# Split weights in a ring whose places begin 64 bytes further, modulo 512, from one to the next

## The chip, the cores and the metric

The kernel runs on one core of one Trainium2 chip. The metric is the device time of one execution in microseconds. Three runs of the kernel before took 1205.24, 1208.13 and 1209.83 us (median 1208.13).

## The reference

Two layers over 512 latent tokens of width 1024, with 256 context tokens. Layer 0 mixes tokens by windowed grouped-query attention (16 heads of 64), layer 1 by a short gated convolution. Each layer ends with a ConvFFN of width 2816. Cut to what carries the time:

```python
def short_conv_mixer(a, w_in, conv_w, w_out):
    gate_b, gate_c, u = jnp.split(a @ w_in, 3, axis=-1)
    return (gate_b * dwconv3(gate_c * u, conv_w)) @ w_out

def conv_ffn(a, w_up, conv_w, w_down):
    g, u = jnp.split(dwconv3(a @ w_up, conv_w), 2, axis=-1)
    return (jax.nn.silu(g) * u) @ w_down

# every layer, latent tokens
sh1, sc1, g1, sh2, sc2, g2 = adaln(c, ada_w[i], ada_b[i])
h = h + g1 * mixer(modulate(rms_norm(h, norm_mix[i]), sh1, sc1))
h = h + g2 * conv_ffn(modulate(rms_norm(h, norm_ffn[i]), sh2, sc2), ffn_w_up[i], ffn_conv[i], ffn_w_down[i])
```

All inputs and the output are float32.

## The kernel before

Activations stand transposed, features on the 128 partitions and tokens along the free dimension. Each float32 operand of a large product is split in two parts of type `fp32r`: `hi` is the rounded value, `lo` what is left. A product of one 128x128 block of weights with 512 (or 256) tokens is then three matmuls, `mm3` (L198 to L201): `hi` x `hi`, `hi` x `lo`, `lo` x `hi`. Each of them loads its block of weights anew; the block is 128 columns of 4 bytes, 512 bytes on each partition.

Weights come from HBM in pieces of 128x1024 (4096 bytes on each partition). `wraw` (L173) loads a piece on SP's queue into one of four buffers. `wpiece` (L180) then splits it: ScalarE writes `whi` (L167), VectorE writes `wlo` (L168). These two go to a ring of places. Ring A has four places for `whi` and four for `wlo` in the pool `ring`; from the FFN pool on, ring B adds three of each, and the pieces use the seven in turn. In the start and in attention pieces of `wqkv` are split into ring A, and there they are the streamed operand (L285 to L287) and the activations are the loaded one.

Ahead of these rings stands the pool `const`: `par`, a tile `pad` that nothing reads, `ident`, `ones`, small columns; then `work` with the 4 buffers of `t` and the 18 of `g`; then `ring` with 4 `wraw`, 4 `whi`, 4 `wlo`. Pools of the stages follow: `e`, then `start` and later `attn`, which are closed before the FFN pool opens in their room. The FFN pool holds `h` (8), ring B (3 `whi`, 3 `wlo`), `crow`, `f` (10), `a` (16), `araw` (3), in this order of addresses. Tiles are laid one behind the other, and so the size of `pad` sets where all that follow in `const`, `work` and `ring` begin.

The order of the work is written out in `START` and `ORDER` for the first layer's attention; from the FFN pool on it is the order of the loops in `out_proj`, `ffn` and the short convolution. `proj` (L721) runs the 24 matmuls of one output block of 128 features. During the first layer's FFN GpSimd and ScalarE compute the second layer's modulation columns from `araw` tiles (L696, L708), two tiles for each step of the FFN.

The lines of before that the change touches:

```python
PAD = 176
    cp.tile([P, PAD], F32, name="pad")
        hi = p.tile([P, 1024], F32R, tag="whi" + t, name=nm("whi"), bufs=nb)
        lo = p.tile([P, 1024], F32R, tag="wlo" + t, name=nm("wlo"), bufs=nb)
```

Of the kernel before, what the change touches and what calls it, by code (L numbers as in the profile page):

```python
# [8 lines left out]
F32R = mybir.dt.float32r  # L9
# [5 lines left out]
P = 128  # L15
# [16 lines left out]
WIN0 = (0, 0, 1, 2)  # L32
WINN = (4, 5, 5, 4)
MASK0 = (5, 2, 2, 0)
HOOK_AT = 6
HALF_AT = 2
KEY_BLOCKS = ((0, 2), (0, 3), (0, 4), (0, 4), (1, 4), (2, 4))
# [8 lines left out]
NPC = _n  # L46
NPC0 = PC["gffn"][0]
NPC1 = PC["qn"][0]
PAD = 176

# [44 lines left out]
def kernel(ctx: ExitStack, tc: tile.TileContext, xT, ctxT, par_d, rope_d, mask_d, ident_d,  # L97
# [11 lines left out]
    def nm(s):  # L109
        uid[0] += 1  # L110
        return f"{s}{uid[0]}"
# [30 lines left out]
    par = cp.tile([P, NPC1], F32, name="par")  # L142
    cp.tile([P, PAD], F32, name="pad")
    ident = cp.tile([P, P], F32, name="ident")
# [21 lines left out]
    def split(raw, hi, lo):  # L166
        act.copy(out=hi, in_=raw)  # L167
        vec.tensor_tensor(out=lo, in0=raw, in1=hi.bitcast(F32), op=ALU.subtract)  # L168
# [4 lines left out]
    def wraw(src, n=1024):  # L173
        raw = rg.tile([P, 1024], F32, tag="wraw", name=nm("wraw"), bufs=4)
        sp.dma_start(out=raw[:, :n], in_=src)
        return raw
# [3 lines left out]
    def wpiece(src, n=1024, raw=None):  # L180
        raw = wraw(src, n) if raw is None else raw
        p, t = ring_pools[wcount[0] % len(ring_pools)]
        nb = sum(r[1] == t for r in ring_pools)
        wcount[0] += 1
        hi = p.tile([P, 1024], F32R, tag="whi" + t, name=nm("whi"), bufs=nb)
        lo = p.tile([P, 1024], F32R, tag="wlo" + t, name=nm("wlo"), bufs=nb)
        parts = 1
        if splits[0] > 0:
            splits[0] -= 1
        elif splits[1] > 0:  # L190
            splits[1] -= 1
            parts = 2
        for i in range(0, n, n // parts):
            cl = slice(i, i + n // parts)
            split(raw[:, cl], hi[:, cl], lo[:, cl])
        return hi, lo
# [71 lines left out]
    with ExitStack() as attn:  # L268
# [22 lines left out]
        with tc.tile_pool(name="start", bufs=1, reuse_waits="tile") as st:  # L291
# [36 lines left out]
            def split_w(i):  # L328
                kvw.append(wpiece(None, 1024, kvraw[i]))
# [234 lines left out]
        def M(p, b, t):  # L564
            e, s = es[p, b, t]
            n = WINN[b] * P
            np_, w = (1, 512) if n == 512 else (2, 320)
            mb = mask[:, MASK0[b]:MASK0[b] + WINN[b], :].rearrange("p a b -> p (a b)")
            h = 2 * p + t
# [114 lines left out]
    with tc.tile_pool(name="ffn", bufs=1, reuse_waits="tile") as fp, four_banks() as sp3:  # L684
# [36 lines left out]
        def proj(pieces, ah, al, halves=False, group=None, hook=None):  # L721
# [5 lines left out]
            for hf in (HALVES if halves else (FULL,)):  # L727
                for m0 in range(0, n, group):
                    for kt in range(nk):
                        if hook is not None and kt == HOOK_AT and hf.start == 0:  # L730
                            hook()
# [12 lines left out]
        for m in range(KT):  # L744
            t = fp.tile([P, 512], F32, tag="h", name=nm("h"), bufs=8)
# [14 lines left out]
        def out_proj(src, n, ah, al, gate, nxt=None, last=False, lead=(), tail_w=None, after=None, cols=None):  # L760
# [15 lines left out]
            for m in range(len(lead), KT - tail):  # L776
                ps = proj([wpiece(src(m), n)], ah, al)[0]
                residual(m, ps, gate)
                done(m, FULL)
                if after is not None:  # L780
                    after(1)
            if not tail:
                return
            ms = list(range(KT - tail, KT))
            pieces = [wpiece(src(m), n) for m in ms] if tail_w is None else tail_w
            banks = [nbank() for m in ms]
            for hf in HALVES:
# [172 lines left out]
```

## Time and profile before

| | |
|---|---|
| runs, us | 1205.24, 1208.13, 1209.83 |
| profiled execution, us | 1207.7 |
| its span, us | 1205.8 |
| mean granted TensorE clock | 0.996 |
| TensorE busy, us | 1184.6 |
| weight loads busy, us | 975.8 |
| VectorE busy, us | 752.1 |
| ScalarE busy, us | 536.9 |
| GpSimd busy, us | 297.2 |
| read from HBM, MB | 152.86 |

The profile is of one execution. PE is TensorE's matmuls, PEld its weight loads, DVE VectorE, ACT ScalarE, POOL GpSimd, SP the engine whose queue issues the transfers. In a row of a group of instructions stand the line, the engine, the operation, the written tile and the read ones, the shapes and the count, then the busy time in us and the mean duration in ns, then the idle time ahead of them and what ended it. For matmuls the duration is that of the whole pipeline, so that matmuls overlap; their rate is read from the distance between the starts in the timeline, whose first two columns are start and duration in us.

### The profile page before, as it was taken

The numbers are of one execution on the slowest core, as the hardware profiler recorded it, in microseconds if no ns is written. First come the engines' busy times: TensorE is split into PE (matmuls) and PEld (weight loads), VectorE is DVE, ScalarE is ACT, GpSimd is POOL, SyncE is SP. The second block draws the span as 40 slices with busy tenths as digits, with TensorE's granted clock in tenths as the row PEclk, the third lists the DMA queues.
The fourth block names the chain that finished last, engine by engine and source line by source line (L and its number), as shares of the span: only waits on it lengthen the run. The fifth ranks groups of instructions, "written<-read, shape, count | busy, mean of one in ns | idle before, by whom it ended". The sixth has DMA issues, their size and how long they took to land.

```text
span 1205.8 us, 16342 instructions
## 1 busy us (share of the span) xinstructions
PE 1184.6 (98%) x6366; PEld 975.8 (81%) x6366; DVE 752.1 (62%) x1107; ACT 536.9 (45%) x899; POOL 297.2 (25%) x204
## 2 busy tenths in 40 slices
PE   8998999999999999999999999999999999999998
PEld 6676666689887888878889988889988888888888
DVE  3688788737777667765776644446676446543652
ACT  4434777634655445644554422324443234422430
POOL 0059688710244543363431000010000000000000
PEclk8999999999999999999999999999999999999999
DMA  9445143153165656566443243332153333323211
GB/s 366 168 156 167 61 149 114 54 192 118 57 245 193 212 155 202 192 213 179 163 134 106 75 135 91 102 92 66 37 174 105 88 105 88 105 89 104 75 31 71
DMA packets 50461, 157.60 MB, mean 131 GB/s; under 512 B 5712, under 2 KB 8016, under 8 KB 50384
## 3 DMA queue, kind: packets, MB, share of 16 engines
q1 hardware_dynamic: 50384, 156.56, 40.3%
q8 instruction: 50, 0.82, 0.3%
q14 instruction: 27, 0.22, 0.1%
HBM read 152.86 MB, written 2.10 MB: 129 GB/s over the span
## 4 chain that ended last, share of the span: by engine, by line
PE 84%; DVE 8%; ACT 3%; issue 2%; POOL 1%; DMA 1%; SPq 0%; POOLq 0%; ACTq 0%; DVEq 0%
PE ps_s L199 11%; PE ps_s L201 11%; PE ps_s L200 11%; PE ps_pt L199 6%; PE ps_pt L200 6%; PE ps_pt L201 6%; DVE wlo L168 3%; PE ps_oa L641 3%; PE ps_pt L622 3%; PE ps_oa L199 3%; PE ps_oa L200 3%; PE ps_oa L201 3%; PE ps_qt L201 3%; PE ps_qt L200 3%; PE ps_qt L199 3%; PE ps_s L561 3%
## 5 line engine op out<-in xcount | busy, mean ns | idle before, releaser
L168 DVE TENSOR_TENSOR wlo<-wraw,whi 128x1024 fp32r<-128x1024 f32 (+2 forms) x194 | 263.2, 1365 | 166.1 <-ACT whi L167 160.7
L167 ACT CAST whi<-wraw 128x1024 fp32r<-128x1024 f32 (+2 forms) x194 | 183.4, 953 | 291.1 <-PE ps_s L200 119.5
L696 POOL TENSOR_TENSOR araw<-araw,crow 128x1024 f32<-128x1024 f32 x56 | 145.2, 2602 | 210.2 <-DMA araw<-in_adat 99.9
L199 PE MATMUL ps_s<-a,whi 128*128 128x512 f32 (+1 forms) x448 | 167.6, 374 | 0.0
L200 PE MATMUL ps_s<-a,whi 128*128 128x512 f32 (+1 forms) x448 | 167.6, 374 | 0.0
L201 PE MATMUL ps_s<-a,wlo 128*128 128x512 f32 (+1 forms) x448 | 167.5, 374 | 0.0
L199 PE MATMUL ps_pt<-a,whi 128*128 128x512 f32 (+1 forms) x272 | 99.1, 364 | 0.0
L201 PE MATMUL ps_pt<-a,wlo 128*128 128x512 f32 (+1 forms) x272 | 99.1, 364 | 0.0
L200 PE MATMUL ps_pt<-a,whi 128*128 128x512 f32 (+1 forms) x272 | 99.0, 364 | 0.0
L199 PE MATMUL ps_s<-g,whi 128*128 128x512 f32 (+1 forms) x264 | 94.5, 358 | 3.0 <-ACT g L167 3.0
L200 PEld LDWEIGHTS ps_s<-a,whi 128*128 128x128 f32 x448 | 84.4, 188 | 14.9
L201 PEld LDWEIGHTS ps_s<-a,wlo 128*128 128x128 f32 x448 | 84.4, 188 | 15.0
L199 PEld LDWEIGHTS ps_s<-a,whi 128*128 128x128 f32 x448 | 84.4, 188 | 14.9
L201 PE MATMUL ps_s<-g,wlo 128*128 128x512 f32 (+1 forms) x264 | 94.3, 358 | 0.0
L200 PE MATMUL ps_s<-g,whi 128*128 128x512 f32 (+1 forms) x264 | 94.1, 357 | 0.0
L167 ACT CAST g<-f 128x512 fp32r<-128x512 f32 x52 | 32.2, 620 | 101.4 <-DVE f L828 100.8
L750 DVE SCALAR_TENSOR_TENSOR h<-ps_s,ada,h 128x512 f32<-128x512 f32 (+1 forms) x40 | 26.6, 670 | 76.2 <-PE ps_s L201 76.2
L827 ACT ACTIVATE f<-f 128x512 f32<-128x512 f32 x44 | 27.9, 633 | 81.9 <-DVE f L741 81.8
L708 ACT ACTIVATE araw<-araw 128x1024 f32<-128x1024 f32 x56 | 58.8, 1052 | 4.0 <-POOL araw L696 4.0
L570 DVE CUSTOM_DVE_ANT_0 e<-ps_s,mask,nsink 128x640 f32<-128x640 f32 (+1 forms) x64 | 53.7, 875 | 10.7 <-PE ps_s L561 10.2
L199 PEld LDWEIGHTS ps_s<-g,whi 128*128 128x128 f32 x264 | 49.8, 189 | 11.1 <-ACT g L167 4.0
L200 PEld LDWEIGHTS ps_pt<-a,whi 128*128 128x128 f32 x272 | 51.3, 189 | 8.1
(297 smaller groups left out, 2619.5 us busy)
## 6 DMA issues: line engine op xcount, KB each, us to landing
wraw<-in_wup SPq DMA_DIRECT2D x88, 512.0 KB, 3.5
araw<-in_adat SPq DMA_DIRECT2D x56, 512.0 KB, 4.4
wraw<-in_wdown SPq DMA_DIRECT2D x32, 512.0 KB, 3.6
araw<-in_ada SPq DMA_DIRECT2D x48, 256.0 KB, 2.8
wraw<-in_wsc SPq DMA_DIRECT2D x24, 512.0 KB, 3.5
gw<-in_ada SPq DMA_DIRECT2D x16, 512.0 KB, 8.9
wraw<-in_wqkv SPq DMA_DIRECT2D x12, 512.0 KB, 6.0
wraw<-in_wdown SPq DMA_DIRECT2D x16, 384.0 KB, 3.1
```

Source lines behind the costliest of these rows:

```text
L167: act.copy(out=hi, in_=raw)
L168: vec.tensor_tensor(out=lo, in0=raw, in1=hi.bitcast(F32), op=ALU.subtract)
L199: pe.matmul(out=ps, lhsT=wh, rhs=ah, start=start, stop=False)
L200: pe.matmul(out=ps, lhsT=wh, rhs=al, start=False, stop=False)
L201: lastmm[0] = pe.matmul(out=ps, lhsT=wl, rhs=ah, start=False, stop=stop)
L561: pe.matmul(out=s[t][:, i, :w], lhsT=q2s[p][x][HALF[t], cl], rhs=KEYS[p // 4][(p // 2 + t) % 2][y][HALF[t], ks_], start=(n == 0), stop=(n ...
L570: vec.tensor_tensor_reduce(out=e[:, :n].rearrange("p (a b) -> p a b", a=np_), in0=s[:, :np_, :w], in1=mb.rearrange("p (a b) -> p a b", a=n ...
L622: pe.transpose(out=pt[:, q:q + P], in_=es[p, b, t][0][:, o:o + P], identity=ident)
L641: pe.matmul(out=r["po"][HALF[t], b0:b0 + n], lhsT=V[:, j, p // 2, :], rhs=pf[:, t * n:(t + 1) * n], start=first, stop=not r["left"])
L696: ins = pool.tensor_tensor(out=w, in0=w, in1=crow, op=ALU.mult)
L708: pace(act.activation(out=w, in_=w, func=AF.Copy, accum_out=col[:, m:m + 1]), after)
L827: act.activation(out=cv[0], in_=cv[0], func=AF.Silu)
```

## The change

Each place of the two tiles that hold split weights gets 16 more float32 columns (64 bytes) that nothing writes or reads: 4160 bytes in place of 4096. The pad shrinks by 128 columns (512 bytes).

```diff
+SKEW = 16
...
-PAD = 176
+PAD = 48
...
-        hi = p.tile([P, 1024], F32R, tag="whi" + t, name=nm("whi"), bufs=nb)
-        lo = p.tile([P, 1024], F32R, tag="wlo" + t, name=nm("wlo"), bufs=nb)
+        hi = p.tile([P, 1024 + SKEW], F32R, tag="whi" + t, name=nm("whi"), bufs=nb)
+        lo = p.tile([P, 1024 + SKEW], F32R, tag="wlo" + t, name=nm("wlo"), bufs=nb)
```

The instructions, their order and the semaphores that they wait for are the same in both programs, on every engine. What differs is where tiles begin on each partition. Ring A has eight places, so it grows by 512 bytes, as much as the pad loses; the pools behind it begin where they did. Ring B has six and grows by 384 bytes, which moves the tiles of the FFN pool behind it. The start of the tiles modulo 512, in bytes:

| tiles | before | after |
|---|---|---|
| `ident`, `ones` | 320 | 320 |
| `t`, `g`, `wraw` | 0 | 0 |
| `whi`, ring A | 0, 0, 0, 0 | 0, 64, 128, 192 |
| `wlo`, ring A | 0, 0, 0, 0 | 256, 320, 384, 448 |
| `whi`, ring B | 0, 0, 0 | 64, 128, 192 |
| `wlo`, ring B | 0, 0, 0 | 192, 256, 320 |
| `h`, `e`, `x`, `pf` | 0 | 0 |
| `crow`, `f`, `a`, `araw` of the FFN pool | 0 | 384 |
| K, V, `qr` of attention | 64 | 64 |
| `q`, `R`, `adaacc`, `araw` of attention | 320 | 320 |
| `gw` of the start | 32 | 32 |

The last tile of attention, `R`, ends at 229,184 bytes of the partition, before and after.

## The prediction

> **What bounds the kernel now.** I read the page first, then busy time by stretch, then the timeline of TensorE. The page gives span, load and the chain that ended last.
>
> ```profile
> span 1205.8 us, 16342 instructions
> PE 1184.6 (98%) x6366; PEld 975.8 (81%) x6366; DVE 752.1 (62%) x1107; ACT 536.9 (45%) x899; POOL 297.2 (25%) x204
> PE 84%; DVE 8%; ACT 3%; issue 2%; POOL 1%; DMA 1%; SPq 0%; POOLq 0%; ACTq 0%; DVEq 0%
> ```
>
> TensorE holds 84% of the chain. Three stretches of the second layer, and then the first matmul line of `mm3` over the whole span (columns: stretch, PE busy, PEld busy, and in the first fence DVE, ACT, POOL; clock, DMA share, GB/s):
>
> ```profile
> 700.00:800.00 100.00, 100.00 (x443) 82.81 (x442) 43.37 (x50) 30.12 (x38) 0.00 (x0) 1.00 0.32 98
> 900.00:1000.00 100.00, 100.00 (x443) 82.56 (x442) 50.33 (x59) 31.78 (x40) 0.00 (x0) 1.00 0.33 100
> 1000.00:1100.00 100.00, 100.00 (x442) 82.58 (x441) 53.79 (x63) 34.44 (x43) 0.00 (x0) 1.00 0.32 95
> ```
> ```profile
> 0.00:1205.80 1205.80, 572.93 (x1584) 298.91 (x1584) 1.00 0.41 131
> ```
>
> There is no idle time at a granted clock of 1.00, so these stretches last as long as their matmuls do: 100 us over 443 is 225.7 ns each. L199, L200 and L201 stand 1584 times each, together 4752 matmuls, each with a weight load of its own out of `whi` or `wlo`. So the time is nearly a count times the distance between starts, and the question is whether this distance (I call it the pitch) hangs on where the weights lie. The other engines have 38% and more of the span free. 0.5% of 1207.7 us is 6.0 us, that is 1.27 ns of pitch; faster or slower below means by more than that, about what a measurement of this kernel can tell from no change.
>
> The pitch has two parts. First and last row of a run of matmuls over 512 columns, then of one over 256; all weights, `a` and `g` tiles lie at 0 modulo 512 bytes here:
>
> ```profile
> 744.78 0.39 PE L201 MATMUL ps_qt<-a,wlo 128*128 128x512 f32 x1
> ...
> 746.82 0.39 PE L201 MATMUL ps_qt<-a,wlo 128*128 128x512 f32 x1
> ```
> ```profile
> 269.77 0.28 PE L201 MATMUL ps_qt<-g,wlo 128*128 128x256 f32 x1
> ...
> 270.97 0.28 PE L199 MATMUL ps_qt<-g,whi 128*128 128x256 f32 x1
> ```
>
> Nine steps in 2.04 us are 226.7 ns; ten steps in 1.20 us are 120.0 ns. So a column costs (226.7 - 120.0)/256 = 0.417 ns, and 120.0 - 256 x 0.417 = 13.3 ns is left for each change of weights, whatever the width. Those 13.3 ns are all that the place of the weights could govern: 4752 x 13.3 = 63 us.
>
> **The change part by part.** It adds no instruction and moves none: on every engine and queue the rows and their waits stand in the same order. It changes addresses alone. `par`, then 704 bytes of pad, made every large tile of the rings begin at 0 modulo 512. With 192 bytes of pad `t`, `g` and `wraw` lie 512 bytes lower, again at 0. The `whi` places of ring A come to 0, 64, 128, 192, its `wlo` places to 256, 320, 384, 448; ring B to 64, 128, 192 and 192, 256, 320. Behind ring B, `crow`, `f`, `a` and `araw` of the FFN pool come to 384. `h` and all tiles of the start and of attention stay.
>
> *Weight loads and streamed operands.* Before has one place where this can be read: the scores L561 take weights from `q` (320 modulo 512) and stream K (64 modulo 512), in pairs that run at once on 64 rows each. First and last `K..h` or `K..l` start of four such groups, behind each group's first pair:
>
> ```profile
> 137.72 0.31 PE L561 MATMUL ps_s<-K0ah,q 64*128 64x320 f32 x1
> ...
> 138.16 0.31 PE L561 MATMUL ps_s<-K0ah,q 64*128 64x320 f32 x1
> ```
> ```profile
> 141.13 0.30 PE L561 MATMUL ps_s<-K0bh,q 64*128 64x320 f32 x1
> ...
> 141.72 0.31 PE L561 MATMUL ps_s<-K0bl,q 64*128 64x320 f32 x1
> ```
> ```profile
> 177.59 0.30 PE L561 MATMUL ps_s<-K1ah,q 64*128 64x320 f32 x1
> ...
> 178.17 0.31 PE L561 MATMUL ps_s<-K1al,q 64*128 64x320 f32 x1
> ```
> ```profile
> 191.91 0.31 PE L561 MATMUL ps_s<-K1ah,q 64*128 64x320 f32 x1
> ...
> 192.49 0.31 PE L561 MATMUL ps_s<-K1al,q 64*128 64x320 f32 x1
> ```
>
> They are 3, 4, 4 and 4 steps in 0.44, 0.59, 0.58 and 0.58 us: 15 steps in 2.19 us, 146.0 ns. The line through the two aligned pitches gives 13.3 + 320 x 0.417 = 146.7 ns. Operands at 64 and 320 cost what operands at 0 and 0 cost, within the rounding of eight printed starts, about 1 ns. The loads themselves:
>
> ```profile
> L199 PEld LDWEIGHTS ps_s<-a,whi 128*128 128x128 f32 x448 | 84.4, 188 | 14.9
> L622 PEld LDWEIGHTS ps_pt<-ident,e 128*128 128x128 f32 x288 | 30.9, 141 | 15.6 <-issue 10.7 <-ACT pf L626 1.5 <-ACT e L576 0.9
> L561 PEld LDWEIGHTS ps_s<-K0ah,q 64*128 64x128 f32 x48 | 7.4, 184 | 2.1 <-issue 1.7 <-DVE q L543 0.2 <-DVE nmx L570 0.2
> L536 PEld LDWEIGHTS ps_qt<-ident,qr 128*128 128x128 f32 x32 | 3.6, 140 | 2.4 <-POOL qr L527 1.7 <-issue 0.6
> L250 PEld LDWEIGHTS ps_qt<-ident,adaacc 128*128 128x128 f32 x16 | 1.8, 141 | 0.8 <-issue 0.8
> ```
>
> Among the transposes `e` lies at 0, `qr` at 64, `adaacc` at 320: 141, 140, 141 ns. In the split format 188 at 0 and 184 at 320. I take 0 for this term, with 1 ns either way as its bounds: 4752 x 1 ns, 5 us down or up. It is the term that is not hidden.
>
> *The split and the work around it.* Two inputs in SBUF, with the same offset and with another one, and results written at 0 and at 320:
>
> ```profile
> L168 DVE TENSOR_TENSOR g<-f,g 128x512 fp32r<-128x512 f32 x52 | 35.9, 690 | 26.4 <-ACT g L167 26.4
> L645 DVE TENSOR_TENSOR t<-ps_oa,R 128x512 f32<-128x512 f32 x8 | 5.5, 687 | 3.0 <-PE ps_oa L641 3.0
> L543 DVE TENSOR_TENSOR q<-ps_qt,q 128x512 fp32r<-128x512 f32 x8 | 5.5, 684 | 1.0 <-ACT q L540 1.0
> L606 ACT COPY R<-ps_qt 128x512 f32<-128x512 f32 x8 | 4.7, 583 | 3.8 <-PE ps_qt L602 3.8
> L880 ACT COPY f<-ps_pt 128x512 f32<-128x512 f32 x3 | 1.7, 579 | 0.0
> L246 POOL TENSOR_TENSOR adaacc<-adaacc,araw 128x512 f32<-128x512 f32 x28 | 36.0, 1286 | 2.3
> L246 POOL TENSOR_TENSOR g<-g,araw 128x512 f32<-128x512 f32 x14 | 18.0, 1288 | 1.2
> ```
>
> VectorE takes 690 ns when both inputs lie at 0 and 684 to 687 with one of them in PSUM and the other at 320; ScalarE writes to 320 in 583 and to 0 in 579; GpSimd adds at 320 and 320 in 1286, at 0 and 320 in 1288. The largest difference, 6 ns, for 194 splits is 1.2 us, and in the stretches quoted above it lies under TensorE. The split of 1024 columns is twice as long in one stretch (450 to 600 us) as in another (700 to 800 us):
>
> ```profile
> L168 DVE TENSOR_TENSOR wlo<-wraw,whi 128x1024 fp32r<-128x1024 f32 x26 | 55.9, 2151 | 22.0 <-ACT whi L167 21.2
> ```
> ```profile
> L168 DVE TENSOR_TENSOR wlo<-wraw,whi 128x1024 fp32r<-128x1024 f32 x19 | 23.3, 1225 | 23.9 <-ACT whi L167 22.9
> ```
>
> The same tiles have the same offsets in both; what differs is GpSimd, which works on `araw` in the one and does nothing in the other (0.00 busy above). So this stretching is no matter of places, and stays. Term: 0, bounds 2 us either way.
>
> *Transfers.* `wraw` stays at 0. `araw` of the FFN goes from 0 to 384.
>
> ```profile
> wraw<-in_wup SPq DMA_DIRECT2D x88, 512.0 KB, 3.5
> araw<-in_adat SPq DMA_DIRECT2D x56, 512.0 KB, 4.4
> araw<-in_ada SPq DMA_DIRECT2D x48, 256.0 KB, 2.8
> gw<-in_ada SPq DMA_DIRECT2D x16, 512.0 KB, 8.9
> wraw<-in_wdown SPq DMA_DIRECT2D x16, 384.0 KB, 3.1
> ```
>
> From 512 and 384 KB at 0 (3.5 and 3.1 us) 256 KB would take 2.7; at 320 they take 2.8. Behind it come the multiplication and the sum of an `araw` tile:
>
> ```profile
> L696 POOL TENSOR_TENSOR araw<-araw,crow 128x1024 f32<-128x1024 f32 x56 | 145.2, 2602 | 210.2 <-DMA araw<-in_adat 99.9
> L708 ACT ACTIVATE araw<-araw 128x1024 f32<-128x1024 f32 x56 | 58.8, 1052 | 4.0 <-POOL araw L696 4.0
> ```
>
> Were an `araw` tile as late as `gw` (8.9 us, at 32, when the program starts and all queues are full), its three buffers would still turn over 3 tiles in 8.9 + 2.6 + 1.1 us (landing, L696, L708), 4.2 us a tile; one step of the FFN (two `proj` of 24 matmuls) asks for two tiles in 48 x 226.7 ns = 10.9 us. Hidden; without that cover L696 would be late and hold SP's queue, and `wraw` behind it.
>
> Sum: 1207.7 us (the profiled execution: span 1205.8 and 1.9 around it) + 0 + 0 + 0, bounds -7 and +7. The runs' median is 1208.13, with 1205.24 to 1209.83. I say **1208 us**, and 1202 to 1214 as this case's own range.
>
> **The rivals.** *Faster: the 13.3 ns are a collision* of the load with the running stream, both at 0 modulo 512, and other offsets end it. It would be worth up to 63 us, 1145 us; a fifth of it would be seen as 13 us, 1195. For it speaks that the cost comes with every change of weights and that every operand of `mm3` has the same offset. Against it, L561 pays it in full with offsets 256 bytes apart. Chance 0.09.
> The Trainium skill (TensorE: Matmul & The Clock Gate, "Wait — 56ns, not 53.3ns?") gives back-to-back matmuls a fixed cost of about 2.5 ns over the columns, not 13. By it some 10.8 ns a matmul could be removable, an estimate of 51 us from that page, 1156 us. The same skill (SBUF — State Buffer, "Who interferes with whom") says that TensorE waits for no other engine's access and gives its loads a read port of their own; by that nothing is removable, and the trace's 146.0 against 146.7 ns agrees with it.
>
> *Slower: a load that crosses a 512-byte line is read in two pieces.* A block of 128 columns is 512 bytes; at 0 it lies in one line, at 64 to 448 in two. All places but the first `whi` cross, about 0.9 of 4752 loads, 4300. If the second piece costs the 13.3 ns once more, this is 57 us, 1265 us; it decides from 1.4 ns a load (6.0 us over 4300). For it: the L561 loads are on 64 rows only, and pairs may hide a part. Against it: those cross as well, at 320, and take 184 ns, and `qr` and `adaacc` cross on 128 rows and take 140 and 141. Chance 0.07.
>
> *The change does nothing to collisions even if there are some*, since both operands run on through all offsets within one matmul (2048 bytes streamed, 512 loaded), and a shift of the start moves a collision rather than ends it: 1208 us, the forecast's time, and a part of its 0.84.
>
> **How the numbers follow.** Forecast 0.84, faster rival 0.09, slower rival 0.07. Of the forecast's share 0.01 falls beyond 0.5% on each side by scatter of the runs: faster 0.10, same 0.82, slower 0.08. The range takes the bounds of the sum and a little of the rivals' weak forms: 1201 to 1215.
>
> **What would show it.** In the profile after: 226.7 and 120.0 ns of pitch again, 442 or 443 matmuls in 100 us of the second layer, weight loads of 188 ns, L168 at 1225 ns between 700 and 800 us. A pitch below 225 or above 228 shows a rival right, and by how much; a changed time at the same pitch would have to come from idle time of TensorE, and would make my account of the bound wrong.

## The result, and the profile after

The changed kernel is slower: 1218.19 us (median of 4 runs, 1217.93 to 1219.41) against 1207.18 us (4 runs of the kernel before), a ratio of 1.0089 with a 95% interval of 1.0074 to 1.0104. I had forecast 1208 us and no change, with 0.08 for slower. The profiled execution has a span of 1216.0 us, 10.2 us more than before.

The page of the changed kernel (lines of the code are one higher than before):

```profile
span 1216.0 us, 16342 instructions
PE 1195.4 (98%) x6366; PEld 973.2 (80%) x6366; DVE 752.6 (62%) x1107; ACT 537.7 (44%) x899; POOL 297.9 (24%) x204
PE 91%; DVE 3%; POOL 2%; issue 2%; ACT 1%; DMA 0%; SPq 0%; POOLq 0%; DVEq 0%; ACTq 0%
```

The time is all on TensorE: 10.8 us more busy, with the same 6366 matmuls. VectorE, ScalarE and GpSimd changed by 0.8 us at most. The same stretches of the second layer as before (stretch, then busy time and count of PE, PEld, DVE, ACT, POOL, then clock, DMA share, GB/s):

```profile
700.00:800.00 100.00, 100.00 (x435) 81.39 (x434) 42.64 (x49) 29.06 (x37) 0.00 (x0) 1.00 0.32 101
900.00:1000.00 100.00, 100.00 (x435) 81.37 (x434) 49.15 (x57) 31.26 (x39) 0.00 (x0) 1.00 0.32 95
1000.00:1100.00 100.00, 100.00 (x435) 81.36 (x434) 53.85 (x63) 35.06 (x45) 0.00 (x0) 1.00 0.32 96
```

There is still no idle time and the granted clock is 1.00, but 435 matmuls fit in 100 us where 443 did: 229.9 ns each, not 225.7. The steps have also become uneven: before, nine tenths of those over 512 columns took 226 or 227 ns, now nine tenths lie between 226 and 238. The first, the last and three in the middle of twelve starts:

```profile
905.83 0.40 PE L202 MATMUL ps_pt<-a,wlo 128*128 128x512 f32 x1
...
907.22 0.40 PE L202 MATMUL ps_pt<-a,wlo 128*128 128x512 f32 x1
907.46 0.40 PE L200 MATMUL ps_qt<-a,whi 128*128 128x512 f32 x1
907.70 0.39 PE L201 MATMUL ps_qt<-a,whi 128*128 128x512 f32 x1
...
908.39 0.39 PE L201 MATMUL ps_qt<-a,whi 128*128 128x512 f32 x1
```

Eleven steps in 2.56 us are 232.7 ns. Over all `mm3` matmuls whose next start is less than 245 ns (512 columns) or 140 ns (256 columns) away, the mean step is 230.96 ns and 118.2 ns, before 226.76 and 119.9 ns. So 512 columns lost 4.2 ns and 256 columns gained 1.7 ns: 3491 x 4.2 - 1228 x 1.7 = 12.6 us. From the first `mm3` matmul to the last it is 976.0 us instead of 964.3, 11.7 us; what else lies in this stretch became 0.9 us shorter. The duration of a weight load, a row that I had relied on, did not move:

```profile
L200 PEld LDWEIGHTS ps_s<-a,whi 128*128 128x128 f32 x448 | 84.3, 188 | 16.4
```

### The profile page after: what moved, and what is told of

It reads as the page before. It is cut to its first block, busy times and chain, and to the rows that moved or that the text cites. A ratio compares the mean times of both kernels' runs of the same rounds, so it can differ in the third digit from the quotient of the medians.

```text
span 1216.0 us, 16342 instructions
## 1 busy us (share of the span) xinstructions
PE 1195.4 (98%) x6366; PEld 973.2 (80%) x6366; DVE 752.6 (62%) x1107; ACT 537.7 (44%) x899; POOL 297.9 (24%) x204
## 4 chain that ended last, share of the span: by engine, by line
PE 91%; DVE 3%; POOL 2%; issue 2%; ACT 1%; DMA 0%; SPq 0%; POOLq 0%; DVEq 0%; ACTq 0%
PE ps_s L202 12%; PE ps_s L200 12%; PE ps_s L201 12%; PE ps_pt L201 7%; PE ps_pt L202 7%; PE ps_pt L200 7%; PE ps_qt L201 3%; PE ps_qt L200 3%; PE ps_qt L202 3%; PE ps_oa L200 3%; PE ps_oa L201 3%; PE ps_oa L202 3%; PE ps_oa L642 3%; PE ps_pt L623 3%; PE ps_s L562 2%
```

## The experiments

No run leaves out any part of the computation. In each, the instructions and their waits are those of before, save where the text says otherwise. By *distance* I mean the address of the block of weights that is loaded less the address of the operand that is streamed, in bytes, modulo 256.

### Which part of the change, and which theory

Theory A: the pitch is set by that distance. Theory B is the slower rival of the prediction: a block that crosses a 512-byte line costs by itself. C and D are other parts of the change: C the tiles that moved to 384, D the differences between the places of successive loads.

One row of the table ahead of the prediction, `whi` of ring B, does not agree with the rest of it: six places of 4160 bytes laid one behind the other from 0 begin at 0, 64, 128 (`whi`) and 192, 256, 320 (`wlo`) and end at 384, where `crow` stands. Nothing below rests on that row.

**The skew with the streams at 0.** 128 bytes behind ring B bring `a` and its neighbours back to 0.

```diff
 the change, and
+        fp.tile([P, 32], F32, name="fill")
         crow = fp.tile([P, 1024], F32, name="crow")
```

> The change, with 128 bytes of fill behind ring B, so that crow, f, a and araw of the FFN pool begin at 0 modulo 512 again: streamed operands all at 0, the places of the weights still spread over 0 to 448. Theory A (the pitch of a 512-column matmul is set by the distance, modulo 256 bytes, between the block of weights that is loaded and the operand that is streamed): places at 0 and 256 are clean, the others not, about as many as in the change: pitch 229 to 232 ns, time 1213 to 1221 us. Theory B (a block that crosses a 512-byte line costs by itself, whatever the stream): the same time as the change, 1218. Theory C (it is the moved a, f, crow and araw that cost): back to 1207.

Measured: 1218.77 us, ratio 1.0102 (1.0087 to 1.0117), pitches 230.8 and 118.0 ns. The move of `a` to 384 is not the cause (C falls). A, B and D are left.

**All weights at one offset.** A tile ahead of the first place and one behind the last of each ring; the places themselves stay 4096 bytes apart.

```diff
+HI_AT = 16      # columns: 64 bytes; in other runs 8, 32, 48, 56, 64
+LO_AT = 16
-PAD = 176
+PAD = 48
+        if new:
+            shift(p, HI_AT)
         hi = p.tile([P, 1024], F32R, tag="whi" + t, name=nm("whi"), bufs=nb)
+        if new:
+            shift(p, (LO_AT - HI_AT) % 128)
         lo = p.tile([P, 1024], F32R, tag="wlo" + t, name=nm("wlo"), bufs=nb)
+        if new:
+            shift(p, -LO_AT % 128)
```

At 64 bytes:

> All fourteen places of split weights at 64 modulo 512, none spread; all streamed operands at 0; pad 48. Theory A (distance modulo 256): every load is at distance 64; loads at that distance in the profile of the change stand at 233 ns for 512 columns and 118 for 256, so 3500 x 6.2 ns more and 1250 x 2.5 less, 1207 + 19 = 1226 us. Theory B (crossing a 512-byte line): all loads cross, 1207 + 4750 x 2.5 ns (the 11 us of the change over its 4300 crossing loads), 1219 us, at both widths alike. Theory D (successive loads from places with different offsets cost): no difference between places, 1207 us.

Measured: 1222.79 us, ratio 1.0136 (1.0121 to 1.0151). The same stretches, and then first and last of twelve starts over 512 columns and of fourteen over 256:

```profile
700.00:800.00 100.00, 100.00 (x430) 80.60 (x429) 42.47 (x48) 28.93 (x36) 0.00 (x0) 1.00 0.34 103
900.00:1000.00 100.00, 100.00 (x431) 80.53 (x430) 48.84 (x56) 30.18 (x38) 0.00 (x0) 1.00 0.31 95
```
```profile
905.70 0.40 PE L214 MATMUL ps_pt<-a,whi 128*128 128x512 f32 x1
...
908.27 0.39 PE L216 MATMUL ps_pt<-a,wlo 128*128 128x512 f32 x1
```
```profile
270.31 0.28 PE L216 MATMUL ps_qt<-g,wlo 128*128 128x256 f32 x1
...
271.79 0.28 PE L214 MATMUL ps_s<-g,whi 128*128 128x256 f32 x1
```

Eleven steps in 2.57 us, 233.6 ns; thirteen in 1.48 us, 113.8 ns (all of the trace: 233.3 and 115.1). There is no difference between places here, and it is slower than the change: D falls as the cause. A gave 233 and 118 ns and 1226 us: over 256 columns the gain is larger than that, and so the time is 3 us shorter. B, with one price at both widths, does not explain that 256 columns become faster.

At 256 bytes:

> All fourteen places of split weights at 256 modulo 512, none spread; all streamed operands at 0; pad 48. Theory A (distance modulo 256): clean, pitch 226.7 and 120 ns, 1207 us. The same with modulo 512 instead: slower by 5 us or more. Theory B (crossing a 512-byte line): 1219 us. Theory D (differences between places): 1207 us.

Measured: 1207.35 us, ratio 1.0000 (0.9990 to 1.0009), pitches 226.8 and 119.9 ns.

```profile
700.00:800.00 100.00, 100.00 (x443) 82.81 (x442) 43.64 (x50) 30.41 (x38) 0.00 (x0) 1.00 0.32 98
900.00:1000.00 100.00, 100.00 (x442) 82.53 (x442) 50.37 (x58) 32.05 (x40) 0.00 (x0) 1.00 0.32 99
```

Every block crosses a 512-byte line and nothing is lost: B falls, and the smaller pad, which this kernel has, costs nothing either. The period of A is 256, not 512.

**Everything at 64**, weights and streams alike:

```diff
-PAD = 176
+PAD = 192
```

> The kernel before with a pad of 192 instead of 176 columns: every tile behind the pad, weights and streams alike, lies 64 bytes further, so all of them at 64 modulo 512 and none at a distance from another. Theory A (distance): as before, 1207 us and 226.7 ns. Theory B (crossing a 512-byte line): all loads cross, 1219 us.

Measured: 1207.99 us, ratio 1.0010 (1.0001 to 1.0019), pitches 226.8 and 119.9 ns, 443 matmuls in the first of these stretches (the 1 us more is not in the pitch):

```profile
700.00:800.00 100.00, 100.00 (x443) 82.81 (x442) 42.45 (x48) 29.02 (x37) 0.00 (x0) 1.00 0.32 101
```

So the place of the weights alone does not set the step; their distance from the streamed operand does.

### Other distances

The same edit with other offsets.

> As the run with all weights at 64, but all at 128 modulo 512, streams at 0. Theory A1 (the cost falls with the distance's size as in the mixed places of the change, where loads at 128 stood at 232.1 and 118.2 ns): 1207 + 3490 x 5.3 - 1225 x 1.7 ns, 1223 us. Theory A2 (any distance that is no multiple of 256 costs the same, 233.3 and 115.1 ns): 1223 us with those pitches. A period of 128 instead of 256: 226.8 and 119.9 ns, 1207 us.

> All weights at 192 modulo 512, streams at 0. Theory A1 (as in the mixed places of the change, 230.1 and 117.0 ns at this distance): 1207 + 3490 x 3.3 - 1225 x 2.9 ns, 1215 us. Theory A2 (all such distances alike, 233.3 and 115.1 ns): 1223 us.

> All weights at 32 modulo 512, streams at 0. If what counts is the 64-byte unit in which a block begins, 32 bytes change nothing: 226.8 and 119.9 ns, 1207 us. If any distance counts, as at 64: about 233 and 115 ns, 1223 us.

> All weights at 224 modulo 512, streams at 0. Theory A1 (the cost is small on this side: 192 took 228.9 and 116.9 ns, and 256 is clean): between 192 and 256, 512 columns at 226 to 228 ns and 256 columns at 117 to 119, 1205 to 1210 us. Theory A2 (a block that begins in the middle of a 64-byte unit costs most, as 32 with 233.3 and 118.3 ns): 1227 us.

Steps between starts over the whole trace, and times; each ratio is to runs of before taken together with it (medians 1206.64 to 1207.47 us):

| distance | 512 columns, ns | 256 columns, ns | time, us | ratio (95% interval) |
|---|---|---|---|---|
| 0 (before) | 226.8 | 119.9 | 1206.64 to 1207.47 | |
| 32 | 233.3 | 118.3 | 1227.45 | 1.0166 (1.0148 to 1.0185) |
| 64 | 233.3 | 115.1 | 1222.79 | 1.0136 (1.0121 to 1.0151) |
| 128 | 232.6 | 118.8 | 1225.77 | 1.0152 (1.0134 to 1.0171) |
| 192 | 228.9 | 116.9 | 1212.33 | 1.0037 (1.0022 to 1.0052) |
| 224 | 233.3 | 116.7 | 1224.71 | 1.0148 (1.0130 to 1.0167) |
| 256 | 226.8 | 119.9 | 1207.35 | 1.0000 (0.9990 to 1.0009) |

At 32, 64 and 224 the step over 512 columns is the same 233.3 ns, 128 is just below, and only 192 is nearer to the aligned one. That 192 costs less does not come from a smaller shift (A1): 224 is nearer to 256 and costs as much as 64, where A1 gave it 1205 to 1210 us. A 64-byte unit alone (32 as good as 0) is refuted too. Over 256 columns every distance other than 0 and 256 is a little faster than 0, by 1.1 to 4.8 ns. What sets the order among the distances stays open.

### Is it the distance, with its sign?

Here the weights stay at 0, and only `crow`, `f`, `a`, `araw` move, by 64 and by 192 bytes.

```diff
+        fp.tile([P, 16], F32, name="fill")      # 48 in the second run
         crow = fp.tile([P, 1024], F32, name="crow")
```

> The kernel before with 64 bytes of fill behind ring B: crow, f, a and araw of the FFN pool begin at 64 modulo 512, all weights and g stay at 0, pad 176. 2400 matmuls over 512 columns and 576 over 256 stream a, so their weights lie at -64, that is 192, modulo 256 from the stream. Theory S (the signed distance weights minus stream modulo 256 counts): as with all weights at 192, 228.9 and 116.9 ns on a, 1207 + 2400 x 2.2 - 576 x 3.0 ns, 1211 us. Theory U (only the size of the shift counts, whichever operand is shifted): as with all weights at 64, 233.3 and 115.1 ns, 1207 + 15.8 - 2.8, 1220 us. If only the place of the weights counts: 1207 us.

> The same with 192 bytes of fill: a at 192, weights at 0, so 64 modulo 256 from the stream. Theory S: 233.3 and 115.1 ns on a, 1220 us. Theory U: as with all weights at 192, 1211 us. If only the place of the weights counts: 1207 us.

Measured: with `a` at 64 1211.38 us, ratio 1.0039 (1.0026 to 1.0051), and 228.9 and 117.6 ns on `a`; with `a` at 192 1220.67 us, ratio 1.0108 (1.0079 to 1.0137), and 233.3 and 116.1 ns on `a`. On `g`, which did not move, 227 and 119.9 ns in both. For comparison, the steps over 256 columns on `a` alone were 117.2 ns with all weights at 192 and 116.4 with all at 64. The stretch from 700 to 800 us, first with `a` at 64, then at 192:

```profile
700.00:800.00 100.00, 100.00 (x439) 82.04 (x438) 42.45 (x48) 28.86 (x36) 0.00 (x0) 1.00 0.32 99
```
```profile
700.00:800.00 100.00, 100.00 (x431) 80.55 (x429) 42.31 (x48) 28.55 (x36) 0.00 (x0) 1.00 0.34 102
```

Theory S gave 1211 and 1220 us. Moving the stream by 64 acts as moving the weights by 192, and the other way round: the signed distance between the two operands counts, whichever of them is moved.

The trace of the change shows this within itself. In ring A the `whi` and the `wlo` of a piece lie at the same offset modulo 256, and the pieces take its four places in turn. With `a` at 0 (the skew with the streams at 0) the matmuls over 512 columns on `a` step by 233.3, 232.7, 228.9 and 226.9 ns in the four places, in the order of use; in the change, with `a` at 384, by 228.9, 226.9, 233.3 and 232.1. These are the table's values for 64, 128, 192, 0, and, 384 bytes less, for 192, 0, 64, 128. (Which place is used first is taken from the values themselves; that the row turns by two places does not depend on it.)

### Two attempts at a gain

Matmuls over 256 columns are faster at a distance. Can this be had for them alone?

**Other cuts.** Every tile stays; the half-width matmuls are cut at column 240 or 272, so that the stream of the second part begins 64 or 192 bytes off.

```diff
+        FIRST = (slice(0, 240), slice(240, T))
+        TAIL = (slice(0, 272), slice(272, T))
-            for hf in (HALVES if halves else (FULL,)):
+            for hf in (FIRST if halves else (FULL,)):
-            for hf in HALVES:
+            for hf in TAIL:
```

> The kernel before, all tiles at 0; only the matmuls that run over half of the tokens are cut at another column: 240 and 272 in the first blocks of a stage, 272 and 240 in its last four, so that the second part's stream begins at 960 or 1088 bytes, a distance of 64 or 192 from the weights modulo 256; no matmul over 512 columns is touched. Theory A: with all weights at 64 matmuls over 256 columns took 115.1 instead of 119.9 ns; the second parts, 612 matmuls, gain 4 to 5 ns each, 2.5 to 3 us, 1204 to 1205 us, and the first parts, aligned, stay on the line (113.3 ns for 240 columns, 126.7 for 272). If a distance costs at any width: 1209 us or more.

Measured: 1209.46 us, ratio 1.0014 (1.0004 to 1.0023): slower by 2 us instead of 3 faster. The pitch did gain, 2.0 us over all half-width matmuls: the first parts took 112.0 ns (240 columns) and 125.4 (272), the second ones 111.7 and 123.4. The aligned first parts, too, were 1.3 ns below the line that the expectation put them on, so not all of the gain is the distance's; the cause of that part is open. But idle time came in behind the parts of 240 columns, which cover the chain of `rstd` for less time. The groups of the transposes L230 (behind the last bar the idle time of TensorE ahead of them), before:

```profile
L230 PE MATMUL ps_s<-ident,rcol 128*128 128x128 f32 x12 | 2.8, 336 | 0.9 <-POOL rcol L224 0.9
L230 PE MATMUL ps_pt<-ident,rcol 128*128 128x128 f32 x4 | 0.9, 298 | 0.5 <-POOL rcol L224 0.5
L230 PE MATMUL ps_qt<-ident,rcol 128*128 128x128 f32 x2 | 0.4, 298 | 0.5 <-POOL rcol L224 0.5
```

and with the other cuts:

```profile
L230 PE MATMUL ps_s<-ident,rcol 128*128 128x128 f32 x12 | 2.8, 341 | 3.5 <-POOL rcol L224 1.8 <-DVE rcol L227 1.7
L230 PE MATMUL ps_pt<-ident,rcol 128*128 128x128 f32 x4 | 0.9, 298 | 1.3 <-POOL rcol L224 1.3
L230 PE MATMUL ps_qt<-ident,rcol 128*128 128x128 f32 x2 | 0.4, 298 | 0.7 <-POOL rcol L224 0.7
```

1.9 us of idle time became 5.5. Some 2.8 us of the 3.6 lie behind second parts of 240 columns, in the tails that stream `g`, the rest behind first parts of 240 columns, on `a`. That the cut parts are too short to cover the chain is read from this order; no run tries it apart.

**A distance of 64 for half-width pieces.** The cuts stay; ring B's places get 256 bytes more, and a piece begins 64 bytes inside its place when it is used over half of the tokens and there is room.

```diff
+        w = 1024 if t == "A" else 1088
+        o = 16 if half and n + 16 <= w else 0
-        hi = p.tile([P, 1024], F32R, tag="whi" + t, name=nm("whi"), bufs=nb)
-        lo = p.tile([P, 1024], F32R, tag="wlo" + t, name=nm("wlo"), bufs=nb)
+        hi = p.tile([P, w], F32R, tag="whi" + t, name=nm("whi"), bufs=nb)[:, o:o + n]
+        lo = p.tile([P, w], F32R, tag="wlo" + t, name=nm("wlo"), bufs=nb)[:, o:o + n]
```

> The kernel before, with 64 bytes of distance for matmuls over 256 columns alone, at the same cuts (256 and 256): ring B's places are 4352 bytes long (0 modulo 256), and a piece that is used over half of the tokens begins 64 bytes inside its place where there is room (ring B, and the pieces of 768 columns): 720 of the 1248 matmuls over 256 columns at distance 64, 3504 over 512 columns at 0. Theory A: those 720 at 115 ns, 720 x 4.8 = 3.5 us of pitch less; since some of them cover the chain that ends in the transposes L230, up to 1.5 us come back as idle time there: 1204 to 1206 us. If all of it comes back, as with the columns cut at 240: 1207.

Measured: 1205.95 us (11 runs) against 1206.64, ratio 0.9992 (0.9983 to 1.0001): no change that these runs can tell. The 720 matmuls took 117.6 ns and not 115.1; 720 x 2.3 ns is 1.7 us. Neighbours at distance 0 are not the reason: by the order in which the pieces take the places, 551 of the 703 steps that can be read have the matmul before and the two behind at distance 64 as well, and those took 117.4 ns. Why they gained only half of what the run with all weights at 64 gave stays open. The idle time ahead of the transposes stayed at 1.9 us. No version beats both kernels clearly.

## Why the prediction was wrong

**What bounds the kernel** was right: no idle time in the stretches shown, before and after, so that the pitch is their time. What the prediction named as the sign of a rival (a pitch above 228) is what came, but by neither rival's mechanism.

**"The pitch has two parts"** was the first wrong step, though not the one that gave the 0. I split 226.7 and 120.0 ns into 0.417 ns a column and a fixed 13.3 ns and took the 13.3 ns for all that the weights' place could govern. With all weights at 64 the two widths give (233.3 - 115.1)/256 = 0.462 ns a column and -3.1 ns fixed. A negative price of a change of weights means that the division does not describe what the distance does: it adds 6.5 ns over 512 columns and takes 4.8 off over 256. A line through two aligned widths could not tell that.

**"Operands at 64 and 320 cost what operands at 0 and 0 cost"** is the step that decided, and it failed. The measurement of L561 was right, but its weights at 320 and its stream at 64 are exactly 256 bytes apart. This is the one distance other than 0 in the table that costs nothing (1207.35 us). I had read two unequal offsets as a test of unequal offsets in general, where it tested a single difference. The width made it blind as well: on a straight line between the two widths of the table (an estimate), 320 columns would take 144.7 to 147.3 ns at the distances that cost, against the 146.7 of my line, so that at 32, 128 or 224 bytes the group would have looked aligned within its 1 ns. The transposes do not help: only the durations of their loads were compared, and such a duration is blind to the effect (188 ns before, after, and with all weights at 32).

**The term "weight loads and streamed operands", 0 with 5 us either way,** measured as +12.6 us by the pitch, +11.7 us from the first `mm3` matmul to the last, +11.0 us in the runs. Its bounds were taken from the rounding of printed starts, as if the only doubt were in the reading.

**The split, the transfers and the rest, 0,** were right as far as it shows: the busy time of no other engine changed by more than 0.8 us, and the median landing of `araw` went from 4.4 to 4.5 us.

**The rivals.** Against the faster one I said that L561 paid the 13.3 ns with offsets 256 bytes apart, which is true and says little, as above. In its general form, that the step depends on where the load lies to the stream, it was right; the aligned state, however, is the better one for 512 columns. The slower rival had the right sign and the wrong mechanism: loads that cross a line cost nothing (everything at 64, weights at 256). The third rival said that a shift of the start only moves a collision, since both operands run through all offsets. That was argued and not measured, and the offset of the starts does count.

The Trainium skill (TensorE: Matmul & The Clock Gate, "Step-by-step: what each phase is for") states that loading the next weights takes no read bandwidth from the running matmul, and (SBUF — State Buffer, "Who interferes with whom") that TensorE's read port for the streamed operand and the one for weight loads are independent. For these matmuls of 4-byte operands the runs show that the addresses of the two are not free of each other: 226.8 against 233.3 ns with nothing but an offset changed, and the measurement decides. Whether the 226.7 ns of before hold a part of such an influence too, no run shows; they are the best of the seven distances tried for 512 columns.

## What to carry to other kernels

When matmuls of 4-byte operands over 512 columns follow each other without idle time and each loads new weights, keep the blocks of weights and the streamed tiles at the same address modulo 256 bytes; a stagger of 64 bytes from place to place cost 0.9% here, all weights 32 bytes off their streams 1.7%. Before an observed pair of offsets is taken for "unaligned costs nothing", look at their difference as well as at each. And a piece of TensorE work that covers another chain can give back what it gains: the cuts at 240 gained 2.0 us of pitch and had 3.6 us more idle time, so cover and pitch belong in one sum.

## What the runs showed of the hardware

- The step between back-to-back matmuls of this kind depends on the signed distance of the two operands modulo 256 bytes: over 512 columns 226.8 ns at 0 and 256, 228.9 at 192, 232.6 to 233.3 at 32, 64, 128 and 224; over 256 columns 119.9 ns at 0, and 115.1 to 118.8 at the others. Moved together, the operands may lie at 0 or at 64: 226.8 ns in both.
- Neither the duration of a weight load (188 ns) nor TensorE's busy share of the span (98% before and after) shows it; the count of matmuls in a stretch without idle time does: 443, 439, 435 or 430 in 100 us.
- Why the period is 256 bytes, why 192 is cheaper than 224, why 256 columns gain where 512 lose, and why they gained less in the last attempt than with all weights at 64, no run here settles.
